# The last token block's gate in pieces of 384 and 128 columns, its output rows weighted early and stored from two queues

## The chip, the cores and the metric

The kernel runs on one core of a Trainium2 chip. The metric is device time in microseconds (us) of one execution. The profiled execution is one further run, recorded by the hardware profiler; its trace is what the rows below come from.

## The reference

One layer of a streaming encoder on 512 tokens with 1024 channels, in float32: a normalised input projection, two attention branches merged by gates, an MLP, then a gated per-layer embedding and a final norm. Only the end of it matters here:

```
ple_gate = sigmoid(rms_norm(h, g_ple) @ w_ple_gate)      # 512x1024 @ 1024x1024
h   = h + ple_gate * (p @ w_ple_proj)
out = rms_norm(h, g_final)                               # h * rsqrt(mean(h*h) + eps) * g_final
```

The output, 512 x 1024 float32, is 2 MB.

## The kernel before

The 512 tokens are four blocks of 128 (`NT` = 4; `LT` = 3 is the last one), one token to a partition. A float32 product is made of three matmuls in a 4-byte format that TensorE takes at full rate: each operand is split into a high and a low part, and `mm3` (lines 74 to 76) adds high x high, high x low and low x high in PSUM.

The gate product of a block is made for 512 columns at a time: 8 slices of the contraction x 3 matmuls = 24 matmuls of 512 columns, each with its own 128x128 weight load (the tokens are the stationary operand). First all four blocks' columns 0 to 511, then columns 512 to 1023 of blocks 0, 1 and 2 (`psgt` in the profile). The last block's columns 512 to 1023 are made in two pieces of 256 (`gate_piece`, `psgl` in the profile), each of 24 matmuls.

What follows a piece (`merge`, `merge_ssq`):

- ScalarE (ACT): sigmoid of the PSUM piece, scaled by the row factor of the earlier norm (line 1398).
- VectorE (DVE): times the projected embedding `pp` (line 1399), then added into `h_sb` (line 1400).
- ACT: square of the new `h_sb` with the row sum into one column of `acc4[tb]` (line 1404, an ACTIVATE and a short read of the accumulator).

`finish(tb)` ends a block: GpSimd (POOL) makes the factor `rs` = (sum + eps)^-0.5 in two small operations (`rms_rstd`, lines 359 and 362), DVE multiplies `h_sb`, `rs` and the broadcast weights `gb4` in one instruction for each half row (line 1423), and SyncE (SP) stores each half, 256 KB (line 1425). The last block has its own end: its first 512 columns are multiplied by `gb4` early (line 1442); when `rs` is there (lines 1452 and 1454), DVE scales those 512 columns (line 1456), then multiplies columns 512 to 767 by both (line 1458); ACT scales columns 768 to 1023 (line 1461) and DVE multiplies these by `gb4` (line 1462). SP stores the two halves (lines 1457 and 1463).

Here the order of instructions on PE, POOL, ACT and DVE is that of the program text (`manual_schedule`). In that text `finish(LT - 1)`, the end of block 2, stands between the first and the second piece of the last block. Line 1488 is the program's closing part, where the engines wait for the last stores and for each other.

Of the kernel before, what the change touches and what calls it, by code (L numbers as in the profile page):

```python
# [8 lines left out]
F32 = mybir.dt.float32  # L9
F32R = mybir.dt.float32r  # L10
AF = mybir.ActivationFunctionType
ALU = mybir.AluOpType
PSUM = bass.MemoryType.PSUM

P = 128
S = 512
# [34 lines left out]
def layer_kernel(ctx: ExitStack, tc: tile.TileContext, x, p, g_mix, w_in, b_forget, swa_sinks,  # L51
                 w_br_swa, w_br_fox, w_mix_out, g_mlp, w_ff1, w_ff2, g_ple, w_ple_gate,
                 w_ple_proj, g_final, out):
    nc = tc.nc
# [3 lines left out]
    out = out[0]  # L58
# [820 lines left out]
    def mm_tile(name, tg=None):  # L879
        if tg is None:  # L880
            n_mm[0] += 1
            tg = ("mm", "sc", "sc", "mm", "sc")[n_mm[0] % 5]
        return psA.tile([P, S], F32, tag=tg, bufs=2 if tg == "mm" else 3, name=name)
# [344 lines left out]
    u3 = {}  # L1228
# [162 lines left out]
    gb4 = hp.tile([P, D], F32, tag="gb", bufs=1, name="g_final_bc")  # L1391
    bcast_row(gb4, g_final)

    def merge(tb, ps, c0, n):

        sl = slice(c0, c0 + n)
        sg = wk3.tile([P, S], F32, tag="tmp", bufs=7, name=f"sgp_{tb}_{c0}")
        nc.scalar.activation(sg[:, 0:n], ps, AF.Sigmoid, scale=rs3[:, tb:tb + 1])  # L1398
        nc.vector.tensor_tensor(sg[:, 0:n], sg[:, 0:n], pp[tb][:, sl], ALU.mult)  # L1399
        nc.vector.tensor_tensor(h_sb[:, tb, sl], h_sb[:, tb, sl], sg[:, 0:n], ALU.add)  # L1400
        return sg
# [2 lines left out]
        nc.scalar.activation(sg[:, 0:n], h_sb[:, tb, c0:c0 + n], AF.Square, scale=1.0 / 32,  # L1404
                             accum_out=acc4[tb][:, col:col + 1])

    def gate_piece(tb, q):

        ts_ = slice(tb * P, (tb + 1) * P)
        ps = mm_tile(f"psgl_{q}")  # L1410
        for k in range(KT):
            wh, wl = unit(("pg", 1, k // 2))
            sl = slice(q * 256, q * 256 + 256)
            mm3(ps[:, 0:256], u3["h"][:, k, ts_], u3["l"][:, k, ts_], wh[:, k % 2, sl],
                wl[:, k % 2, sl], k == 0, k == KT - 1)
        return ps[:, 0:256]

    def finish(tb):
        o = wk3.tile([P, D], F32, tag="xn", bufs=2, name=f"o_{tb}")
# [14 lines left out]
    with tc.manual_schedule(engines={ET.Activation, ET.DVE}):  # L1434
        for tb in range(LT):
            ps = row_group("psgt", "pg", u3_t, 1, tb)
            if tb > 0:
                finish(tb - 1)
            sg = merge(tb, ps, 512, 512)
            merge_ssq(tb, sg, 512, 512, 1)  # L1440
        o = wk3.tile([P, D], F32, tag="xn", bufs=2, name=f"o_{LT}")
        nc.vector.tensor_tensor(o[:, 0:512], h_sb[:, LT, 0:512], gb4[:, 0:512], ALU.mult)
        ps0, ps1 = gate_piece(LT, 0), gate_piece(LT, 1)
        sg = merge(LT, ps0, 512, 256)
        merge_ssq(LT, sg, 512, 256, 1)
        finish(LT - 1)
        acc = acc4[LT]
        nc.vector.tensor_tensor(acc[:, 0:1], acc[:, 0:1], acc[:, 1:2], ALU.add)
        sg = merge(LT, ps1, 768, 256)
        merge_ssq(LT, sg, 768, 256, 2)  # L1450
        ms = sm.tile([P, 1], F32, tag="ms", name="n4_l_ms")
        nc.gpsimd.tensor_scalar(ms, acc[:, 0:1], acc[:, 2:3], EPS, ALU.add, ALU.add)
        rs = sm.tile([P, 1], F32, tag="rs", name="n4_l_rs")
        nc.gpsimd.tensor_tensor(rs, ms, mhalf, ALU.pow)
        rows_ = slice(LT * P, (LT + 1) * P)
        nc.vector.tensor_scalar(o[:, 0:512], o[:, 0:512], rs, None, ALU.mult)
        nc.sync.dma_start(out[rows_, 0:512], o[:, 0:512])
        nc.vector.scalar_tensor_tensor(o[:, 512:768], h_sb[:, LT, 512:768], rs, gb4[:, 512:768],
                                       ALU.mult, ALU.mult)
        hg = sg[:, 256:512]  # L1460
        nc.scalar.activation(hg, h_sb[:, LT, 768:1024], AF.Copy, scale=rs)
        nc.vector.tensor_tensor(o[:, 768:1024], hg, gb4[:, 768:1024], ALU.mult)
        nc.sync.dma_start(out[rows_, 512:1024], o[:, 512:1024])


# [27 lines left out]
```

## Time and profile before

| | us |
|---|---|
| median of 3 runs (lowest, highest) | 721.35 (721.29, 721.50) |
| profiled execution | 721.84 |
| its span, first to last instruction | 720.1 |
| PE busy in the span | 705.6 (98%) |
| DVE, ACT, POOL busy | 531.5, 449.4, 87.6 |

1.74 us of the profiled execution lie outside its span. A line of a timeline gives the start in the span, the duration, the engine, the line of the kernel, the operation, and output <- inputs. "SPq" and "ACTq" are the instruction queues of SyncE and ScalarE, from which stores are issued. A busy PE is not PE at its peak, since the ends of matmuls are modelled.

### The profile page before, as it was taken

The numbers are of one execution on the slowest core, as the hardware profiler recorded it, in microseconds if no ns is written. First come the engines' busy times: TensorE is split into PE (matmuls) and PEld (weight loads), VectorE is DVE, ScalarE is ACT, GpSimd is POOL, SyncE is SP. The second block draws the span as 40 slices with busy tenths as digits, with TensorE's granted clock in tenths as the row PEclk, the third lists the DMA queues.
The fourth block names the chain that finished last, engine by engine and source line by source line (L and its number), as shares of the span: only waits on it lengthen the run. The fifth ranks groups of instructions, "written<-read, shape, count | busy, mean of one in ns | idle before, by whom it ended". The sixth has DMA issues, their size and how long they took to land.

```text
span 720.1 us, 11455 instructions
## 1 busy us (share of the span) xinstructions
PE 705.6 (98%) x4229; PEld 626.6 (87%) x4229; DVE 531.5 (74%) x900; ACT 449.4 (62%) x836; POOL 87.6 (12%) x127
## 2 busy tenths in 40 slices
PE   7999999999999999999999999999999999999995
PEld 6988888888888998888899789988999889988884
DVE  5567888877696556545879985899679966997564
ACT  5547888779863553344777646874578546866452
POOL 1011211100001200002410102010300020010101
PEclk9999999999999999999999999999999999999998
DMA  9256456670364894450995598739994689079002
GB/s 290 65 155 159 109 136 154 150 197 1 118 206 116 152 339 162 160 173 11 252 220 202 105 285 168 235 87 254 190 259 113 157 234 227 31 147 349 1 30 87
DMA packets 74055, 116.72 MB, mean 162 GB/s; under 512 B 6664, under 2 KB 44048, under 8 KB 74000
## 3 DMA queue, kind: packets, MB, share of 16 engines
q1 hardware_dynamic: 65792, 86.38, 37.9%
q0 software_dynamic: 8064, 29.36, 22.2%
q8 instruction: 33, 0.54, 0.3%
q10 hardware_dynamic: 144, 0.26, 0.1%
q14 instruction: 22, 0.18, 0.1%
HBM read 72.93 MB, written 4.19 MB: 107 GB/s over the span
## 4 chain that ended last, share of the span: by engine, by line
PE 85%; DVE 9%; ACT 2%; issue 2%; DMA 1%; POOL 0%; POOLq 0%; DVEq 0%; ACTq 0%
PE pf L74 5%; PE pf L76 5%; PE pf L75 5%; PE s_6x L1309 3%; PE s_4x L1309 3%; PE s_0x L1309 3%; PE s_2x L1309 3%; PE h_sc L752 2%; PE h_pv L822 2%; PE h_tr L810 2%; PE psy L75 2%; PE psy L76 2%; PE psy L74 2%; PE psm L76 2%; PE psm L75 2%; PE psm L74 2%
## 5 line engine op out<-in xcount | busy, mean ns | idle before, releaser
L298 POOL DMA_DIRECT2D wq<-wq x26 | 23.6, 942 | 174.9 <-DVE u154l L325 25.9
L770 ACT ACTIVATE s<-s,h_nm 128x128 f32<-128x128 f32 (+1 forms) x64 | 32.6, 512 | 5.9 <-DVE h_nm L763 5.1
L359 POOL TENSOR_SCALAR n_ms<-acc 128x1 f32<-128x1 f32 x15 | 6.3, 419 | 164.8 <-ACT junk L1075 100.4
L71 DVE TENSOR_TENSOR h_ptl<-h_tr,h_pth 128x512 fp32r<-128x512 f32 (+2 forms) x40 | 22.9, 604 | 3.9 <-ACT h_pth L70 3.6
L467 PE MATMUL va<-wv_h,u 128*128 128x320 f32 x64 | 20.1, 319 | 0.8 <-ACT u L70 0.7
L70 ACT CAST h_pth<-h_tr 128x512 fp32r<-128x512 f32 (+2 forms) x40 | 19.4, 523 | 1.8 <-PE h_tr L810 1.4
L70 ACT CAST u<-n_tr 128x512 fp32r<-128x512 f32 x22 | 12.2, 586 | 13.1 <-PE n_tr L1123 5.9
L810 PE MATMUL h_tr<-ident,s 128*128 128x128 f32 x136 | 19.6, 277 | 0.2
L467 PE MATMUL vb<-wv_h,u 128*128 128x328 f32 x64 | 19.6, 313 | 0.0
L298 POOL DMA_DIRECT2D wgw<-wgw x8 | 7.1, 970 | 101.9 <-DVE u25l L325 77.7
L71 DVE TENSOR_TENSOR u<-n_tr,u 128x512 fp32r<-128x512 f32 x22 | 14.6, 685 | 6.5 <-ACT u L70 6.5
L1075 ACT ACTIVATE junk<-h_sb 128x512 f32<-128x512 f32 x16 | 10.1, 630 | 12.3 <-DVE h_sb L1065 9.8
L822 PE MATMUL h_pv<-h_pth,v 128*128 128x256 f32 (+1 forms) x64 | 17.3, 291 | 0.0
L822 PE MATMUL h_pv<-h_ptl,v 128*128 128x256 f32 (+1 forms) x64 | 16.9, 305 | 0.3 <-DVE h_ptl L71 0.3
L810 PEld LDWEIGHTS h_tr<-ident,s 128*128 128x128 f32 x136 | 15.0, 141 | 2.0 <-ACT s L790 0.5
L1399 DVE TENSOR_TENSOR sgp<-sgp,pp 128x512 f32<-128x512 f32 (+1 forms) x9 | 5.7, 633 | 14.6 <-ACT sgp L1398 14.6
L1065 DVE TENSOR_TENSOR h_sb<-psm,h_sb 128x512 f32<-128x512 f32 x8 | 5.5, 689 | 14.3 <-PE psm L76 14.3
L790 ACT ACTIVATE s<-s,h_rec 128x128 f32<-128x128 f32 (+2 forms) x32 | 14.2, 482 | 2.3 <-DVE h_rec L784 2.3
L832 DVE TENSOR_TENSOR h_ao<-h_pv,h_ao 64x512 f32<-64x512 f32 x16 | 10.9, 681 | 6.1 <-ACT h_ao L831 5.8
L758 DVE CUSTOM_DVE_ANT_0 s<-h_sc,causal 128x128 f32<-128x128 f32 (+3 forms) x32 | 13.8, 482 | 0.3 <-PE h_sc L752 0.3
L784 DVE RECIPROCAL h_rec<-h_den 128x4 f32<-128x4 f32 x16 | 3.0, 185 | 14.5 <-ACT s L770 14.3
L822 PEld LDWEIGHTS h_pv<-h_ptl,v 128*128 128x128 f32 x64 | 12.1, 188 | 1.7 <-DVE h_ptl L71 0.8
(1607 smaller groups left out, 2773.8 us busy)
## 6 DMA issues: line engine op xcount, KB each, us to landing
wq<-in_w_ff_dram SPq DMA_DIRECT2D x45, 512.0 KB, 5.7
wq<-wq POOLq DMA_DIRECT2D x26, 512.0 KB, 5.1
wq_c<-in_w_ff_dram SPq DMA_DIRECT2D x9, 512.0 KB, 5.8
wg<-in_w_in_dram SPq DMA_DIRECT2D x4, 1024.0 KB, 5.4
wgw<-in_w_in_dram SPq DMA_DIRECT2D x8, 512.0 KB, 5.2
wgw<-wgw POOLq DMA_DIRECT2D x8, 512.0 KB, 5.8
wmix<-in_w_mix_out_dram SPq DMA_DIRECT2D x4, 1024.0 KB, 4.9
wpg<-in_w_ple_gate_dram SPq DMA_DIRECT2D x4, 1024.0 KB, 8.6
```

What stands on the lines that cost most here:

```text
L70: nc.scalar.copy(hi, src)
L71: nc.vector.tensor_tensor(lo, src, hi.bitcast(F32), ALU.subtract)
L74: nc.tensor.matmul(ps, lh, rh, start=start, stop=False)
L75: nc.tensor.matmul(ps, lh, rl, start=False, stop=False)
L76: nc.tensor.matmul(ps, ll, rh, start=False, stop=stop)
L298: nc.gpsimd.dma_start(q, other, accum_op=ALU.add)
L467: nc.tensor.matmul(ps, u[:, kk_, ts_], w[:, kk_, c0:c1], start=kk_ == 0 and n == 0, stop=kk_ == KT - 1 and n == 2)
L752: nc.tensor.matmul(ps[:, off:off + n], qs[i][z][:, qb * P:(qb + 1) * P], kk[i][z][:, k0:k0 + n], start=z == 0, stop=z == 1)
L770: nc.scalar.activation(sl, sl, AF.Exp, bias=nm[:, qb:qb + 1], accum_out=den[:, qb:qb + 1])
L810: nc.tensor.transpose(tr[:, n, :], c["s"][:, o, :], ident)
L822: nc.tensor.matmul(pv[:, q0:q0 + nq, :], V2[kb][:, c["v"], :], t[:, o:o + nq, :], start=n == 0, stop=n == 2 * NT - 1, skip_group_check=True)
L1309: nc.tensor.matmul(ps, o[:, j, ts_], w[:, j, :], start=tg != "" and j == 0 and n == 0, stop=j == 1 and n == 2, skip_group_check=True)
```

## The change

The last block's second half of the gate is cut at column 384 instead of 256. `gate`, the sigmoid, is taken out of `merge`, so that the second piece's sigmoid stands ahead of the first piece's square on ACT. Columns 512 to 1023 of the last block's rows are multiplied by `gb4` on DVE piece by piece, before the row factor is known. `finish(LT - 1)` stands behind all of this. When the factor is there, ACT scales columns 0 to 511 and stores them from its own queue, and DVE scales columns 512 to 1023, which SP stores.

```diff
-    def merge(tb, ps, c0, n):
-
-        sl = slice(c0, c0 + n)
+    def gate(tb, ps, c0, n):
         sg = wk3.tile([P, S], F32, tag="tmp", bufs=7, name=f"sgp_{tb}_{c0}")
         nc.scalar.activation(sg[:, 0:n], ps, AF.Sigmoid, scale=rs3[:, tb:tb + 1])
+        return sg
+
+    def merge(tb, ps, c0, n, sg=None):
+
+        sl = slice(c0, c0 + n)
+        if sg is None:
+            sg = gate(tb, ps, c0, n)
...
-    def gate_piece(tb, q):
+    def gate_piece(tb, c0, c1):
...
-        ps = mm_tile(f"psgl_{q}")
+        ps = mm_tile(f"psgl_{c0}")[:, 0:c1 - c0]
...
-        ps0, ps1 = gate_piece(LT, 0), gate_piece(LT, 1)
-        sg = merge(LT, ps0, 512, 256)
-        merge_ssq(LT, sg, 512, 256, 1)
-        finish(LT - 1)
+        C = 384
+        ps0, ps1 = gate_piece(LT, 0, C), gate_piece(LT, C, 512)
+        sg = merge(LT, ps0, 512, C)
+        sg1 = gate(LT, ps1, 512 + C, 512 - C)
+        merge_ssq(LT, sg, 512, C, 1)
+        nc.vector.tensor_tensor(o[:, 512:512 + C], h_sb[:, LT, 512:512 + C], gb4[:, 512:512 + C],
+                                ALU.mult)
+        merge(LT, ps1, 512 + C, 512 - C, sg1)
         acc = acc4[LT]
         nc.vector.tensor_tensor(acc[:, 0:1], acc[:, 0:1], acc[:, 1:2], ALU.add)
-        sg = merge(LT, ps1, 768, 256)
-        merge_ssq(LT, sg, 768, 256, 2)
+        merge_ssq(LT, sg1, 512 + C, 512 - C, 2)
+        nc.vector.tensor_tensor(o[:, 512 + C:], h_sb[:, LT, 512 + C:], gb4[:, 512 + C:], ALU.mult)
+        finish(LT - 1)
...
-        nc.vector.tensor_scalar(o[:, 0:512], o[:, 0:512], rs, None, ALU.mult)
-        nc.sync.dma_start(out[rows_, 0:512], o[:, 0:512])
-        nc.vector.scalar_tensor_tensor(o[:, 512:768], h_sb[:, LT, 512:768], rs, gb4[:, 512:768],
-                                       ALU.mult, ALU.mult)
-        hg = sg[:, 256:512]
-        nc.scalar.activation(hg, h_sb[:, LT, 768:1024], AF.Copy, scale=rs)
-        nc.vector.tensor_tensor(o[:, 768:1024], hg, gb4[:, 768:1024], ALU.mult)
+        nc.scalar.activation(o[:, 0:512], o[:, 0:512], AF.Copy, scale=rs)
+        nc.scalar.dma_start(out[rows_, 0:512], o[:, 0:512])
+        nc.vector.tensor_scalar(o[:, 512:1024], o[:, 512:1024], rs, None, ALU.mult)
         nc.sync.dma_start(out[rows_, 512:1024], o[:, 512:1024])
```

## Rows read from the trace of the kernel before

**Rows 1.** The page, its fourth part: the chain of work that ended last, shares of the span by engine.

```profile
PE 85%; DVE 9%; ACT 2%; issue 2%; DMA 1%; POOL 0%; POOLq 0%; DVEq 0%; ACTq 0%
```

**Rows 2.** The chain that ended last, from 705 us to the end, in order of time: start, duration, engine, output and line. Between the first two rows here lie the other matmuls of the two pieces.

```profile
705.85 0.11 PE psgl L74
...
711.49 0.13 PE psgl L76
...
711.70 0.48 ACT sgp L1398
...
712.21 0.43 DVE sgp L1399
...
712.66 0.43 DVE h_sb L1400
...
713.12 0.52 ACT sgp L1404 x2
...
713.73 0.30 POOL n_l_ms L1452
...
714.07 0.61 POOLq L1488
```

**Rows 3.** The timeline from 707.2 us to the end, all engines; "x2" are two instructions in one row, and its time runs from the first's start to the second's end.

```profile
710.13 1.41 DVE L1423 SCALAR_TENSOR_TENSOR o<-h_sb,n_rs,g_final_bc 128x512 f32<-128x512 f32 x2
...
710.91 0.99 SPq L1425 DMA_DIRECT2D out_dram<-o  x2
...
711.46 0.15 DVE L1448 TENSOR_TENSOR acc<-acc 128x1 f32<-128x1 f32 x1
...
714.71 0.51 ACT L1461 ACTIVATE sgp<-h_sb,n_l_rs 128x256 f32<-128x256 f32 x1 [1.08 <-POOL n_l_rs L1454]
714.71 0.48 DVE L1456 TENSOR_SCALAR o<-o,n_l_rs 128x512 f32<-128x512 f32 x1 [1.62 <-POOL n_l_rs L1454]
715.11 0.48 DVE L1458 SCALAR_TENSOR_TENSOR o<-h_sb,n_l_rs,g_final_bc 128x256 f32<-128x256 f32 x1
715.22 0.33 SPq L1457 DMA_DIRECT2D out_dram<-o  x1
715.51 0.42 DVE L1462 TENSOR_TENSOR o<-sgp,g_final_bc 128x256 f32<-128x256 f32 x1
715.95 0.33 SPq L1463 DMA_DIRECT2D out_dram<-o  x1
```

**Rows 4.** The timeline of an attention head from 195 us, PE and its weight loads (PEld): matmuls of the same 4-byte format, with a new 128x128 weight load each, of 384, 256 and 128 columns, and the first of 512 columns behind them.

```profile
195.40 0.34 PE L822 MATMUL h_pv<-h_pth,v 128*128 128x384 f32 x1
...
195.58 0.34 PE L822 MATMUL h_pv<-h_ptl,v 128*128 128x384 f32 x1
...
195.75 0.28 PE L822 MATMUL h_pv<-h_pth,v 128*128 128x256 f32 x1
...
195.99 0.23 PE L822 MATMUL h_pv<-h_pth,v 128*128 128x128 f32 x1
195.99 0.19 PEld L822 LDWEIGHTS h_pv<-h_ptl,v 128*128 128x128 f32 x1
196.05 0.27 PE L822 MATMUL h_pv<-h_ptl,v 128*128 128x128 f32 x1
196.10 0.19 PEld L74 LDWEIGHTS pf<-u,u18h 128*128 128x128 f32 x1
196.16 0.44 PE L74 MATMUL pf<-u,u18h 128*128 128x512 f32 x1
```

**Rows 5.** The instructions on the sigmoid's tile, 690 us to the end: count, duration in ns (min/median/max), first and last start, and the shapes among them.

```profile
L1399 DVE TENSOR_TENSOR sgp<-sgp,pp x6: 424/691/693, 690.8 to 712.2; 128x512 f32<-128x512 f32 x4, 128x256 f32<-128x256 f32 x2
...
L1404 ACT ACTIVATE sgp<-h_sb x6: 416/632/634, 692.8 to 713.1; 128x512 f32<-128x512 f32 x4, 128x256 f32<-128x256 f32 x2
L1404 ACT ACTIVATION_READ_ACCUMULATOR sgp<-h_sb x6: 185/186/187, 693.3 to 713.4; 128x1 f32 x6
L1398 ACT ACTIVATE sgp<-psgt,rs x4: 670/691/693, 689.9 to 705.9; 128x512 f32<-128x512 f32 x4
L1398 ACT ACTIVATE sgp<-psgl,rs x2: 474/474/475, 708.8 to 711.7; 128x256 f32<-128x256 f32 x2
```

**Rows 6.** Stretches of 0.25 and 1 us around the last four stores: the stretch, its length, busy time of each engine (instructions), then the granted TensorE clock, the mean busy share of the 16 DMA engines and what they moved in GB/s.

```profile
711.50:711.75 0.25, 0.10 (x1) 0.00 (x0) 0.11 (x2) 0.05 (x1) 0.00 (x0) 1.00 0.06 25
...
712.00:713.00 1.00, 0.00 (x0) 0.00 (x0) 0.76 (x2) 0.17 (x1) 0.00 (x0) 1.00 1.01 377
713.00:713.25 0.25, 0.00 (x0) 0.00 (x0) 0.09 (x1) 0.13 (x1) 0.00 (x0) 1.00 0.52 189
716.00:716.25 0.25, 0.00 (x0) 0.00 (x0) 0.00 (x0) 0.00 (x0) 0.00 (x0) 0.68 0.77 295
716.25:717.25 1.00, 0.00 (x0) 0.00 (x0) 0.00 (x0) 0.00 (x0) 0.00 (x0) 0.50 0.97 361
...
717.50:717.75 0.25, 0.00 (x0) 0.00 (x0) 0.00 (x0) 0.00 (x0) 0.00 (x0) 0.50 0.10 33
```

**Rows 7.** The stores of the output rows from 690 us on, from issue to landing.

```profile
DMA to landing us min/median/max: 2.0/2.0/2.1
```

**Rows 8.** The issues of transfers over the whole kernel, the only one from ACT's queue: output <- input, queue, count, size of each, us from issue to landing.

```profile
x<-in_x_dram ACTq DMA_DIRECT2D x1, 256.0 KB, 3.5
```

More of the change, by code (lines that the diff above doesn't have):

```diff
@@ L1405, in merge_ssq @@
                              accum_out=acc4[tb][:, col:col + 1])
-    def gate_piece(tb, q):
+    def gate_piece(tb, c0, c1):
         ts_ = slice(tb * P, (tb + 1) * P)
-        ps = mm_tile(f"psgl_{q}")
+        ps = mm_tile(f"psgl_{c0}")[:, 0:c1 - c0]
         for k in range(KT):
             wh, wl = unit(("pg", 1, k // 2))
-            sl = slice(q * 256, q * 256 + 256)
-            mm3(ps[:, 0:256], u3["h"][:, k, ts_], u3["l"][:, k, ts_], wh[:, k % 2, sl],
+            sl = slice(c0, c1)
+            mm3(ps, u3["h"][:, k, ts_], u3["l"][:, k, ts_], wh[:, k % 2, sl],
                 wl[:, k % 2, sl], k == 0, k == KT - 1)
-        return ps[:, 0:256]
+        return ps
     def finish(tb):
```

## The prediction

> **What bounds the kernel now.** I read the page first. The chain that ended last is 85% PE and 9% DVE [rows 1], so most of the 720 us is matmul time that the change leaves alone. The question is the end: what lies behind the last matmul, and what the change does to the matmuls just before it. The chain in order of time [rows 2] shows PE running without a gap from the first 256-column matmul of the last block (705.85) to the last (711.49 + 0.13 = 711.62): 48 matmuls, 0.12 us each. Then single instructions take turns: sigmoid 711.70, two DVE steps, square 713.12, two POOL steps to 714.68. The timeline [rows 3] has the rest: DVE and ACT start at 714.71 with the factor; the first store is issued at 715.22, the second at 715.95. A store lands 2.0 us after its issue [rows 7], so the second lands at 717.95; 2.15 us of closing part follow, to 720.1.
>
> The view that decides is the stretches around the stores [rows 6]. From 716.25 to 717.25 the DMA engines are busy 0.97 of the time and move 361 GB/s; the pair of block 2's stores before it, issued at 710.91 and 0.66 later [rows 3], shows 1.01 and 377 GB/s. So a pair of 256 KB stores already fills the engines. Block 2's pair moves from about 711.73 (25 of 377 GB/s in the quarter that ends at 711.75) to 713.12 (189 GB/s in the next quarter): 1.39 us, **0.695 us for a store**, first bytes 0.82 us after the issue. The last pair begins at 716.06, 0.84 after its issue, and its last byte is at 717.52 (33 GB/s in the last quarter).
>
> **The change part by part.** I keep one clock, that of the trace.
>
> *Pieces of 384 and 128 columns.* Before: 48 x 0.12 = 5.77 us. The attention head has the same kind of matmul with its own weight load [rows 4]. 384 columns: starts 195.40, 195.58, 195.75, so 0.175 each, 24 x 0.175 = 4.20 us. 128 columns: the first is followed after 0.06 us (195.99 to 196.05), but the second takes 0.27 instead of 0.23 and the next matmul starts 0.11 behind it (196.16), itself lengthened to 0.44. The weight loads beside them start 0.11 apart (195.99, 196.10). I read that as: the first of the pair found its weights loaded behind a longer matmul, the second had to wait for its own, and a row of 24 such matmuls goes at the pace of the weight loads. Bounds: 24 x 0.06 = 1.44 and 24 x 0.12 = 2.88 (the pace at 256 columns, which bounds it from above); I take 0.11, the row's, 2.64 us. Sum 6.84 instead of 5.77: PE ends at 712.69, **1.07 later**.
>
> The Trainium skill bears on this in "TensorE: Matmul & The Clock Gate". Section "LDWEIGHTS (loading the stationary operand)" gives columns / 1.2 in ns, 107 ns for 128 columns, which is the 0.11 of the rows; section "Back-to-back issue gap" gives about 81 ns for a matmul of 128 columns in a stream of load and matmul pairs. By the first the piece would take 24 x 0.107 = 2.57 us, by the second 24 x 0.081 = 1.94 us.
>
> *The chain behind the piece.* The second piece is half as wide. From 512 and 256 columns [rows 5]: sigmoid 0.691 and 0.474, so 0.366 for 128, 0.11 saved; the DVE steps 0.691 and 0.424, so 0.29, 0.13 saved on each of two; square 0.632 and 0.416, so 0.31, 0.11 saved. Together 0.48. The sigmoid starts 1.07 later, at 712.77; the factor is there at 714.68 + 1.07 - 0.48 = 715.27.
>
> *The new wait.* The second piece's sigmoid now waits for PE until 712.77 on ACT; the first piece's square is queued behind it. The first piece's last addition ends at about 711.9 (705.85 + 4.20, sigmoid from 710.13 for 0.58, two DVE steps of 0.56), so the square loses 1.2 us. It runs 713.14 to 713.76 (0.52 and the accumulator read of 0.19, overlapped by about 0.1). The DVE sum of `acc` waits for it, and behind that the rest of DVE; but DVE's own addition for the second piece ends only at 713.78. Cost: nothing, covered by those DVE steps; without that cover, up to 0.6.
>
> *Early weights.* The product of 384 columns (0.56) lies on DVE between 711.9 and the second sigmoid's end at 713.14: hidden; without the gap it would delay the second piece by 0.56. The product of 128 columns (0.29, of which some 0.08 overlaps the next instruction) stands at 713.95, behind the `acc` sum (0.15), in POOL's time; POOL hides it from the factor, but not from what follows on DVE.
>
> *`finish(LT - 1)` moved.* Its factor has long been there; its two DVE instructions now start at about 714.20 instead of 710.13. By the old rows a pair lasts 1.41, the second 0.66 behind the first, and the first store is issued 0.78 after the start, the second 0.66 later [rows 3]. So block 2's stores are issued at **714.98 and 715.64** on SP, not at 710.91 and 711.57. This is all that moves on SP's queue: the last block's store stands behind both. DVE is taken until about 715.6.
>
> *The last pass.* Before: from 714.71 to the second issue 715.95. After: DVE scales 512 columns (0.48) from 715.52, where the second instruction of `finish` lets it in (0.66 behind that one's start at 714.86), 0.25 later than the factor would allow; SP issues at 716.03. ACT scales 512 columns from 715.30; 256 took 0.51 [rows 3], and 0.22 for 256 more by the sigmoid's step [rows 5], so 0.73; ACT issues at about 716.06. If only the issue mattered, the last store would land at 716.06 + 2.0 = 718.06: 0.11 later than before.
>
> *The DMA engines.* But now four stores, 1 MB, are issued between 714.98 and 716.06. First bytes at 714.98 + 0.83 = 715.81, four times 0.695 makes 2.78, so the last byte moves at 718.59; before, at 717.52. All four are issued early enough to keep the engines full (the last may start at 716.9, while two stores last until 717.2). **Sum: +1.07 us.** The share of 1.0 with one queue leaves no room that a second queue could use. No row has stores from two queues at once. The Trainium skill, "DMA: Bandwidth & Descriptors", section "Issuing engines are not separate DMA queues", says that transfers from several issuers run on the same 16 engines and that a second issuer saves only the time to initiate.
>
> So the profiled execution, 721.84, becomes 722.9. It lies 0.49 above the median of the runs; on the median, 721.35 + 1.07 = **722.4**. 0.2%, about what a measurement of this kernel can tell from no change, is 1.44 us.
>
> **The rivals.**
>
> *A. The 128-column matmuls run faster than 0.11.* At the lower bound, 0.06, PE ends at 711.49. The second sigmoid runs 711.57 to 711.94, then DVE's early product of 384 columns is in the way (until about 712.4); the second addition ends at 712.98 instead of 713.78, and all behind it comes 0.8 earlier: block 2's first store at 714.18, last byte at 717.79, +0.27, 721.6. Speaks for it: the one step of 0.06 in the rows; against it: the lengthened matmul behind it. At the 81 ns that the Trainium skill's "Back-to-back issue gap" gives, the addition ends at 713.08 and the sum is about +0.37, 721.7.
>
> *B. Two queues move more than one.* If the stores didn't hold each other up, only the issue would count: +0.11, 721.5. Against it: shares of 0.97 to 1.01 with one queue. With A as well, the last issue at about 715.26 lands at 717.26, 0.7 earlier, 720.7: the only way to a gain, and still under 0.2%.
>
> *C. The store from ACT's queue lands late.* The kernel's only transfer from that queue, a load at the start, took 3.5 us [rows 8]. A store that takes 3.5 from 716.06 lands at 719.56, 1.61 after the old 717.95: 723.0, slower by over 0.2%. It decides from a landing of 719.39 on, 3.33 us after the issue. For it: the row; against it: that is a load, and SP's stores land in 2.0 [rows 7]; but in my sum, where the four stores share the engines, this one takes about 2.9 already.
>
> **How the numbers follow.** My forecast 0.66: 722.4, with a range of its own from 722.0 to 722.8 (0.1 us for the matmul pace up to 0.12, 0.2 for the stores' rate, the rest the runs' own spread). A 0.13, B 0.06 (both at once 0.02 of these), C 0.15. Faster by over 0.2%: 0.03, left for what none of these names. Slower: C but for its milder half-cases, 0.12, and 0.07 of the forecast's and others' upper tail, together 0.19. Within 0.2%: 0.78. The range reaches down to B and A, 721.5, and up to C, 723.1.
>
> **What would show it.** In the profile after: 24 matmuls of 128 columns start 0.11 apart, PE's last ends at about 712.7; ACT's square of 384 columns starts behind the 128-column sigmoid; block 2's DVE pair begins near 714.2; four stores issued within 1.1 us, DMA share about 1 from 715.8 to 718.6, and the closing part as long as before. A PE end at 711.5 speaks for A, a DMA rate over 390 GB/s for B, a store of ACT's queue that lands last and alone for C. The prediction is wrong if block 2's stores are issued before the last block's second addition, if the closing part grows with a second queue in use, or if the stores of two queues slow each other below 361 GB/s: at 0.79 us each instead of 0.695, the sum passes 0.2%.

## The result and the profile after

The changed kernel takes 723.19 us (median of 9 runs, 722.89 to 724.29) beside 721.83 (median of 9, 721.29 to 723.18) of the kernel before in the same session: ratio 1.0023, 95% interval [1.0014, 1.0032], that is +1.66 us [1.0, 2.3]. The two medians by themselves lie 1.36 us apart, inside the same interval. I had forecast 722.4 and a range up to 723.1, and that no difference of 0.2% would show. Part of the miss is the base: the forecast stands on 721.35, the median of three runs, which are the first three of these nine; the same +1.07 on 721.83 is 722.90. What is left is that the direction of my sum was right and its size was too small. The runs below show that two of its steps were wrong and that a third cost was missing.

The profiled execution after: 723.10 us, span 721.06. Everything that follows is told from the first matmul of the last block's pieces, 705.69 before and 705.45 after: the work ahead of it is the same, and in the kernels below it starts anywhere between 704.69 and 705.97. From there to the end of the span ("the stretch") it is 720.12 - 705.69 = 14.43 us before and 721.06 - 705.45 = **15.61 us** after, +1.18 (the trace holds the span to the nanosecond; the views print it to a tenth). Outside the span lie 723.10 - 721.06 = 2.04 us, before 1.72. So the profiled executions differ by 1.18 - 0.24 (the earlier start) + 0.32 = 1.26.

The timeline of the changed kernel, PE's last matmuls and what follows (start, duration, engine, line, operation, output <- inputs); it answers to [rows 2, 3, 4]:

```profile
709.63 0.22 PE L74 MATMUL psgl<-u169h,u 128*128 128x128 f32 x1
709.70 0.27 PE L75 MATMUL psgl<-u169l,u 128*128 128x128 f32 x1
709.81 0.27 PE L76 MATMUL psgl<-u169h,u 128*128 128x128 f32 x1
...
712.15 0.28 PE L76 MATMUL psgl<-u172h,u 128*128 128x128 f32 x1
...
712.52 0.37 ACT L1396 ACTIVATE sgp<-psgl,rs 128x128 f32<-128x128 f32 x1 [2.05 <-PE psgl L76]
712.79 0.51 ACT L1409 ACTIVATE sgp<-h_sb 128x384 f32<-128x384 f32 x1
713.25 0.29 DVE L1405 TENSOR_TENSOR h_sb<-h_sb,sgp 128x128 f32<-128x128 f32 x1
713.46 0.15 DVE L1457 TENSOR_TENSOR acc<-acc 128x1 f32<-128x1 f32 x1
713.58 0.31 ACT L1409 ACTIVATE sgp<-h_sb 128x128 f32<-128x128 f32 x1 [0.18 <-DVE h_sb L1405]
713.79 1.41 DVE L1428 SCALAR_TENSOR_TENSOR o<-h_sb,n_rs,g_final_bc 128x512 f32<-128x512 f32 x2
714.07 0.62 POOL L1462 TENSOR_SCALAR n_l_ms<-acc 128x1 f32<-128x1 f32 x1 [4.48 <-ACT sgp L1409]
714.56 1.00 SPq L1430 DMA_DIRECT2D out_dram<-o  x2
714.78 0.84 POOL L1464 TENSOR_TENSOR n_l_rs<-n_l_ms,mhalf 128x1 f32<-128x1 f32 x1
715.65 0.72 ACT L1466 ACTIVATE o<-o,n_l_rs 128x512 f32<-128x512 f32 x1 [1.68 <-POOL n_l_rs L1464]
715.65 0.49 DVE L1468 TENSOR_SCALAR o<-o,n_l_rs 128x512 f32<-128x512 f32 x1 [0.45 <-POOL n_l_rs L1464]
716.17 0.33 SPq L1469 DMA_DIRECT2D out_dram<-o  x1
716.40 0.35 ACTq L1467 DMA_DIRECT2D out_dram<-o  x1
```

The matmuls of 128 columns start 0.11 us apart, and PE's part, the sigmoid and the two additions stand where the prediction put them. The row to look at is POOL's: its two operations on one number to a partition took 0.62 and 0.84 us, where the same two operations took 0.30 and 0.56 before:

```profile
713.73 0.30 POOL L1452 TENSOR_SCALAR n_l_ms<-acc 128x1 f32<-128x1 f32 x1 [3.90 <-ACT sgp L1404]
714.11 0.56 POOL L1454 TENSOR_TENSOR n_l_rs<-n_l_ms,mhalf 128x1 f32<-128x1 f32 x1
```

Stretches around the four stores, after (columns as in [rows 6]):

```profile
715.25:715.50 0.25, 0.00 (x0) 0.00 (x0) 0.00 (x0) 0.00 (x0) 0.25 (x1) 0.50 0.43 164
...
716.75:717.00 0.25, 0.00 (x0) 0.00 (x0) 0.00 (x0) 0.00 (x0) 0.00 (x0) 0.50 0.20 66
...
717.25:718.25 1.00, 0.00 (x0) 0.00 (x0) 0.00 (x0) 0.00 (x0) 0.00 (x0) 0.50 1.01 389
718.25:718.50 0.25, 0.00 (x0) 0.00 (x0) 0.00 (x0) 0.00 (x0) 0.00 (x0) 0.50 0.53 197
```

The last byte moves at about 718.4; with the earlier start taken off, the prediction's 718.59 is 718.35. That agreement is chance in part: the first bytes move at about 715.4, some 0.2 us earlier than the sum had them (715.81 less 0.24), since DVE's pair begins at 713.79 and not at 714.20 less 0.24. About as much is lost in the quarter at 66 GB/s, because the factor came late and the last two stores with it. And the last byte was not what the end waited for. That is in the closing line's own rows, which the prediction did not use. DRAIN and EVENT_SEMAPHORE are instructions of that line; the second kind carries the signals between the engines. The closing line of the kernel before, its queues (count, duration in ns min/median/max, first and last start):

```profile
L1488 POOLq EVENT_SEMAPHORE  x4: 17/17/17, 719.4 to 720.0; - x4
L1488 POOLq DRAIN  x3: 40/102/5266, 714.1 to 719.9; - x3
L1488 SPq DRAIN  x3: 7/7/7, 718.5 to 719.6; - x3
```

and of the kernel after:

```profile
L1494 POOLq EVENT_SEMAPHORE  x4: 17/17/17, 720.3 to 721.0; - x4
L1494 POOLq DRAIN  x3: 40/93/5542, 714.7 to 720.8; - x3
L1494 SPq DRAIN  x3: 7/7/7, 719.0 to 720.5; - x3
```

SP waits for its stores and reaches its first DRAIN at 718.5 before and 719.0 after. POOL's first DRAIN begins beside its last operation, lasts 5.27 and 5.54 us, and POOL's first signal comes only at 719.4 and 720.3: 0.9 and 1.3 us after SP was through its stores. In both kernels the end of the span lies 5.44 to 5.45 us behind the end of POOL's last operation (714.67 to 720.12; 715.62 to 721.06).

### The profile page after: what moved, and what is told of

The parts are those of the page before. It is cut to its first block, busy times and chain, and to the rows that moved or that the text cites. A ratio compares the mean times of both kernels' runs of the same rounds, so it can differ in the third digit from the quotient of the medians.

```text
span 721.1 us, 11457 instructions
## 1 busy us (share of the span) xinstructions
PE 706.0 (98%) x4229; PEld 627.0 (87%) x4229; DVE 531.3 (74%) x900; ACT 449.2 (62%) x836; POOL 88.2 (12%) x127
## 4 chain that ended last, share of the span: by engine, by line
PE 88%; DVE 7%; DMA 2%; ACT 1%; issue 1%; POOL 0%; SPq 0%; POOLq 0%; DVEq 0%; ACTq 0%
PE pf L74 5%; PE pf L76 5%; PE pf L75 5%; PE s_6x L1309 3%; PE s_4x L1309 3%; PE s_2x L1309 3%; PE s_0x L1309 3%; PE h_sc L752 2%; PE h_pv L822 2%; PE h_tr L810 2%; PE psm L76 2%; PE psm L75 2%; PE psy L74 2%; PE psy L76 2%; PE psm L74 2%; PE psy L75 2%
## 5 line engine op out<-in xcount | busy, mean ns | idle before, releaser
L1404 DVE TENSOR_TENSOR sgp<-sgp,pp 128x512 f32<-128x512 f32 (+2 forms) x9 | 5.7, 632 | 16.1 <-ACT sgp L1396 16.1
L467 PEld LDWEIGHTS va<-wv_h,u 128*128 128x128 f32 x64 | 12.0, 188 | 2.1 <-ACT u L70 1.4
```

Of the source, the lines that this page charges most:

```text
L467: nc.tensor.matmul(ps, u[:, kk_, ts_], w[:, kk_, c0:c1], start=kk_ == 0 and n == 0, stop=kk_ == KT - 1 and n == 2)
```

## The experiments

In every kernel here the numbers are of the profiled execution, the ratio of the timed runs against runs of the kernel before on the same chip. "Outside" is the time outside the span, the median over the runs of that kernel. The ratio is the one on record; it differs by up to 0.0004 from the quotient of the two medians.

| kernel | stretch | POOL's two last operations | end of POOL's last to end of span | outside | ratio [95%] |
|---|---|---|---|---|---|
| before | 14.43 | 0.30, 0.56 | 5.45 | 1.70 | 1 |
| after | 15.61 | 0.62, 0.84 | 5.44 | 2.07 | 1.0023 [1.0014, 1.0032] |
| s1_sp_queue | 15.62 | 0.62, 0.84 | 5.45 | 1.77 | 1.0022 [1.0013, 1.0031] |
| b1_act_queue | 14.43 | 0.30, 0.56 | 5.44 | 2.06 | 1.0004 [0.9995, 1.0012] |
| f1_finish_early | 15.01 | 0.30, 0.56 | 5.44 | 1.88 | 1.0012 [1.0003, 1.0021] |
| p1_psum_scale | 15.01 | 0.30, 0.56 | 5.44 | 2.07 | 1.0009 [1.0000, 1.0018] |
| d1_pool_later | 15.94 | 0.19 (an added one) | 5.44 | 1.71 | 1.0021 [1.0012, 1.0030] |
| d2_store_later | 14.43 | 0.30, 0.56 | 5.45 | 1.73 | 0.9997 [0.9988, 1.0006] |
| k1_pair_only | 15.61 | 0.62, 0.84 | 5.44 | 2.05 | 1.0019 [1.0010, 1.0028] |
| c1_cut_256 | 15.05 | 0.65, 0.84 | 5.45 | 2.05 | 1.0011 [1.0002, 1.0021] |
| v1_weights_early | 14.42 | 0.30, 0.56 | 5.44 | 1.76 | 1.0000 [0.9991, 1.0009] |
| x1_factor_act | 13.59 | none at the end | - | 1.69 | 0.9990 [0.9981, 0.9999] |
| x2_both | 14.58 | none at the end | - | 1.85 | 1.0001 [0.9992, 1.0010] |
| x3_three_stores | 13.60 | none at the end | - | 1.78 | 0.9993 [0.9984, 1.0002] |

### The queue, the place of block 2's end, POOL's neighbours

Four kernels went first, while I still took the end for that of the stores.

**s1_sp_queue**: the changed kernel with all stores on SP.

```diff
         nc.scalar.activation(o[:, 0:512], o[:, 0:512], AF.Copy, scale=rs)
-        nc.scalar.dma_start(out[rows_, 0:512], o[:, 0:512])
         nc.vector.tensor_scalar(o[:, 512:1024], o[:, 512:1024], rs, None, ALU.mult)
         nc.sync.dma_start(out[rows_, 512:1024], o[:, 512:1024])
+        nc.sync.dma_start(out[rows_, 0:512], o[:, 0:512])
```

> The kernel after with one edit: the last block's columns 0 to 511, still scaled on ACT, are stored from SP behind the other half instead of from ACT's queue. In the kernel after, the stretch from the first matmul of the last block's pieces to the end of the span is 15.7 us (14.4 before), the closing part from the last landing to the end 2.3 (2.15 before), and 2.0 to 2.1 us of an execution lie outside its span (1.74 in the profiled one before). Theory: the second queue in use at the end costs 0.15 us of closing part and 0.3 us outside the span; then this kernel has 2.15 and 1.75, its last store is issued at most 0.1 later, and it is 0.3 to 0.4 us faster than the kernel after, ratio to before about 1.0017. Rival: these two differences are chance from one execution to the next; then the kernel stays within 0.1 us of the kernel after, or gets slower by the later issue.

Measured: stretch 15.62 (after 15.61), 1.77 outside the span instead of 2.07, ratio 1.0022. So half of the theory held: the queue changes nothing inside the span, and the 0.3 us outside come off, but are too small to show in the ratio.

**b1_act_queue**: the kernel before with its last store on ACT's queue.

```diff
-        nc.sync.dma_start(out[rows_, 512:1024], o[:, 512:1024])
+        nc.scalar.dma_start(out[rows_, 512:1024], o[:, 512:1024])
```

> The kernel before with one edit: the last store, columns 512 to 1023 of the last block, is issued from ACT's queue instead of SP's. Nothing is computed in another place or order. Theory of the second queue's cost: the closing part grows from 2.15 to 2.3 us and the time outside the span from 1.74 to about 2.05; 0.4 to 0.5 us slower than before in all, ratio 1.0006. Rival (chance): both as before within 0.05 us, ratio 1.000.

Measured: stretch 14.43, as before to the hundredth; outside the span 2.06 (2.01 to 2.11 in 11 runs) instead of 1.70 (1.66 to 1.77 in 32 of before). So the store from ACT's queue costs 0.36 us, all of it outside the span. In the ratio that is 1.0004, within its uncertainty.

**f1_finish_early**: the changed kernel with `finish(LT - 1)` ahead of the last block's two pieces, so that block 2's multiplications and stores come early.

```diff
         ps0, ps1 = gate_piece(LT, 0, C), gate_piece(LT, C, 512)
+        finish(LT - 1)
         sg = merge(LT, ps0, 512, C)
...
         nc.vector.tensor_tensor(o[:, 512 + C:], h_sb[:, LT, 512 + C:], gb4[:, 512 + C:], ALU.mult)
-        finish(LT - 1)
```

> The kernel after with one edit: the end of block 2 (two DVE multiplications and their two stores) stands ahead of the last block's first piece, where DVE is idle for 2.1 us, instead of behind everything. Theory: in the kernel after, each of POOL's two operations for the last factor waits out one of these DVE multiplications, which read two tensors from SBUF (0.62 and 0.84 us instead of 0.30 and 0.56); here they take 0.30 and 0.56 again, the factor comes 0.60 earlier, only two stores are left at the end, and the last byte moves 0.57 earlier: stretch of 15.1 us, ratio to before about 1.0015. The product for the first piece starts 0.45 later on DVE, which costs nothing. Rival (the late stores alone held the end, POOL's operations were long for another reason, such as the work on ACT beside them): POOL's operations stay at 0.62 and 0.84 and the gain is below 0.1 us.

Measured: stretch 15.01, 0.60 less than after; ratio 1.0012. POOL's two operations are short again, in the timeline of f1:

```profile
714.04 0.30 POOL L1462 TENSOR_SCALAR n_l_ms<-acc 128x1 f32<-128x1 f32 x1 [4.48 <-ACT sgp L1409]
714.43 0.56 POOL L1464 TENSOR_TENSOR n_l_rs<-n_l_ms,mhalf 128x1 f32<-128x1 f32 x1
```

But this moves the two late stores and the two late multiplications together, so it doesn't tell them apart.

**p1_psum_scale**: keeps the two late stores, and a late pair of DVE instructions, but not their two inputs from SBUF, the engines' shared memory. Block 2's rows are multiplied by the weights early, into two tiles in PSUM, the memory that TensorE writes; late, DVE only scales these by the factor.

```diff
+        o2 = wk3.tile([P, D], F32, tag="xn", bufs=2, name=f"o_{LT - 1}")
+        rs2 = rms_rstd(acc4[LT - 1], f"n4_{LT - 1}")
+        hg2 = [psA.tile([P, S], F32, tag="tr", bufs=3, name=f"hg_{i}") for i in range(2)]
+        for i in range(2):
+            nc.vector.tensor_tensor(hg2[i], h_sb[:, LT - 1, i * 512:i * 512 + 512],
+                                    gb4[:, i * 512:i * 512 + 512], ALU.mult)
+
+        def finish_late():
+            for i in range(2):
+                s2 = slice(i * 512, i * 512 + 512)
+                nc.vector.tensor_scalar(o2[:, s2], hg2[i], rs2, None, ALU.mult)
+                nc.sync.dma_start(out[(LT - 1) * P:LT * P, s2], o2[:, s2])
+
...
-        finish(LT - 1)
+        finish_late()
```

> The kernel after, with block 2's rows multiplied by the final weights early on DVE into two PSUM tiles; the late step, at the same place as in the kernel after, is a scaling that reads PSUM (one input, no second tensor from SBUF) and writes the rows, and the stores stay late. Theory (a DVE instruction with two SBUF inputs keeps POOL out): POOL's two operations take 0.30 and 0.56 and the factor comes 0.60 earlier than in the kernel after, although DVE is as busy; the four stores then hold the end: the last byte moves at most 0.3 earlier, since 1 MB at 0.695 us for 256 KB has to pass from block 2's first store on. Stretch 15.4 us. Rivals: any DVE work beside POOL slows it (0.62 and 0.84 stay); or the stores don't hold each other up (then the whole 0.57 is gained, stretch 15.1).

Measured: stretch 15.01, ratio 1.0009. DVE's late pair starts at the same place and lasts as long as in the changed kernel, and POOL beside it is not held up:

```profile
713.33 1.40 DVE L1460 TENSOR_SCALAR o<-hg,n_rs 128x512 f32<-128x512 f32 x2
...
713.62 0.30 POOL L1475 TENSOR_SCALAR n_l_ms<-acc 128x1 f32<-128x1 f32 x1 [3.74 <-ACT sgp L1409]
714.01 0.56 POOL L1477 TENSOR_TENSOR n_l_rs<-n_l_ms,mhalf 128x1 f32<-128x1 f32 x1
714.11 0.99 SPq L1461 DMA_DIRECT2D out_dram<-o  x2
```

The same run has the opposite case, earlier: the two products into PSUM, which do read two SBUF inputs, stand beside POOL's first operation for block 2's factor.

```profile
707.86 1.30 DVE L1454 TENSOR_TENSOR hg<-h_sb,g_final_bc 128x512 f32<-128x512 f32 x2
...
708.20 1.04 POOL L359 TENSOR_SCALAR n_ms<-acc 128x1 f32<-128x1 f32 x1 [4.49 <-ACT sgp L1409]
```

It took 1.04 us instead of 0.30. So what goes with the longer time is DVE's two inputs from SBUF, not a busy DVE and not the place of the result.

The length of the stretch didn't fit my theory. The four stores are all late here, their bytes move without a gap, and the last byte comes some 0.4 us later in the stretch than in f1 (about 12.8 against 12.4 us); by the stores p1 had to be the slower one. Yet both end at 15.01. The rival that named 15.1 was near in the number and not in the reason: the four stores do hold each other up, 1 MB moving from 714.9 to 717.8. What the two have in common is POOL's last operation, and that is how the second theory came up: **the end of the span is POOL's last operation plus 5.44 us, and the stores have time to spare.** The rival to it remained that the last landing sets the end.

### Which of the two sets the end

**d1_pool_later**: the kernel before with one more POOL operation behind its last DVE instruction, an addition on 128x1 whose result nobody uses.

```diff
         nc.vector.tensor_tensor(o[:, 768:1024], hg, gb4[:, 768:1024], ALU.mult)
         nc.sync.dma_start(out[rows_, 512:1024], o[:, 512:1024])
+        late = sm.tile([P, 1], F32, tag="ms", name="late")
+        nc.gpsimd.tensor_tensor(late, o[:, 1023:1024], mhalf, ALU.add)
```

> The kernel before with one small operation more: POOL adds a constant to one column of the last block's finished rows (128x1, result unused), so that POOL's last instruction ends some 1.7 us later than before, at about 10.7 us after the first matmul of the last block's pieces instead of 8.98. Nothing else waits for it. Theory (POOL's closing drain ends 4.67 us after POOL's last instruction and, with 0.78 us behind it, sets the end of the execution; the stores have slack): the stretch grows by the same 1.6 to 1.7 us, from 14.4 to 16.1, ratio about 1.0023. Rival, that of the prediction (the last store's landing sets the end): unchanged, 14.4, ratio 1.000.

Measured: POOL's new operation, and the closing line's DRAIN behind it, in the profile of d1:

```profile
715.43 0.19 POOL L1465 TENSOR_TENSOR late<-o,mhalf 128x1 f32<-128x1 f32 x1 [1.33 <-DVE o L1462]
```

```profile
L1490 POOLq DRAIN  x3: 40/93/4889, 715.4 to 720.8; - x3
```

It ends at 715.62, the span at 721.06: 5.44 again. Stretch 15.94, ratio 1.0021. POOL's last operation ends 1.51 us later in the stretch than before, and the stretch is 1.51 longer. An operation of 0.19 us that nothing waits for costs as much as the whole change.

**d2_store_later**: the kernel before with a DVE multiplication into a scratch tile ahead of the last store's producer, so that the store is issued 0.67 us later.

```diff
         nc.scalar.activation(hg, h_sb[:, LT, 768:1024], AF.Copy, scale=rs)
+        scr = wk3.tile([P, S], F32, tag="tmp", bufs=7, name="scr")
+        nc.vector.scalar_tensor_tensor(scr, h_sb[:, LT, 0:512], rs, gb4[:, 0:512], ALU.mult,
+                                       ALU.mult)
         nc.vector.tensor_tensor(o[:, 768:1024], hg, gb4[:, 768:1024], ALU.mult)
```

> The kernel before with one DVE instruction more ahead of the last one: a multiplication of 512 columns into a scratch tile, 0.66 us, so that the last store is issued 0.66 us later. The factor is there by then, POOL has nothing left to do. Rival, that of the prediction (the last store's landing sets the end): the stretch grows by 0.66, from 14.4 to 15.1, ratio 1.0009. Theory (POOL's drain sets the end): SP is through with its waits 0.8 us before the drain ends, so all 0.66 is slack: 14.4, ratio 1.000.

Measured, the two last stores in the timeline of d2:

```profile
714.22 0.33 SPq L1457 DMA_DIRECT2D out_dram<-o  x1
715.62 0.33 SPq L1466 DMA_DIRECT2D out_dram<-o  x1
```

The last store is issued 1.40 us behind the first instead of 0.73 [rows 3], and the stretch is 14.43, the ratio 0.9997: nothing. With d1 this settles it for the kernel before: 0.67 us on the last store are free, and POOL's last operation moves the end one for one.

### The cut and the pair, each by itself

**k1_pair_only**: f1 with two multiplications into scratch tiles in the place where the changed kernel has block 2's; the stores of block 2 stay early.

```diff
+        for i in range(2):
+            scr = wk3.tile([P, S], F32, tag="tmp", bufs=7, name=f"scr_{i}")
+            nc.vector.scalar_tensor_tensor(scr, h_sb[:, LT - 1, i * 512:i * 512 + 512], mhalf,
+                                           gb4[:, i * 512:i * 512 + 512], ALU.mult, ALU.mult)
```

> The kernel with block 2's end moved early, and two DVE multiplications with the same inputs as there, into scratch tiles, at the late place: DVE reads two tensors from SBUF beside POOL's two operations as in the kernel after, but block 2's stores stay early. Theory: POOL's operations take 0.62 and 0.84 us again instead of 0.30 and 0.56, the factor comes 0.60 later than without the pair, and the end with it: stretch 15.6 as in the kernel after, against 15.0 without the pair; so the pair alone, without the stores, is the loss. Rival (the stores of block 2 at the late place lengthen POOL's operations or the end): 0.30 and 0.56, 15.0.

Measured, the timeline of k1:

```profile
714.07 1.41 DVE L1463 SCALAR_TENSOR_TENSOR scr<-h_sb,mhalf,g_final_bc 128x512 f32<-128x512 f32 x2
...
714.36 0.62 POOL L1466 TENSOR_SCALAR n_l_ms<-acc 128x1 f32<-128x1 f32 x1 [4.49 <-ACT sgp L1409]
715.06 0.84 POOL L1468 TENSOR_TENSOR n_l_rs<-n_l_ms,mhalf 128x1 f32<-128x1 f32 x1
```

Stretch 15.61 against 15.01 of f1: the pair alone, without any late store, costs 0.60 us, and it costs it on POOL (0.62 + 0.84 instead of 0.30 + 0.56, +0.60). The two late stores cost nothing (15.61 with and without them).

**c1_cut_256**: the changed kernel with the cut back at 256.

```diff
-        C = 384
+        C = 256
```

> The changed kernel with its last block cut at 256 and 256 columns as before; the four stores, their two queues and the early weights stay. Theory (the end is GpSimd's last operation plus 5.44 us): the last matmul comes 1.07 us earlier, the chain behind it is 0.48 us longer, and the pair of late multiplications on VectorE still holds GpSimd's two small operations up (0.62 and 0.84 us), so GpSimd's power ends some 0.55 us earlier than in the changed kernel: first late matmul to end of span 15.1 us instead of 15.65, outside the span 2.05 us, ratio to before 1.0014. Rival (the four stores set the end): the two late stores come on the same 0.6 us earlier but the transfers of block 2 are still under way, so the end moves by 0.3 us at most, and the closing stretch between the last landing and the end of the span stays as it is in the changed kernel.

Measured: stretch 15.05, ratio 1.0011, POOL 0.65 and 0.84. The cut costs 15.61 - 15.05 = 0.56.

**v1_weights_early**: the kernel before with only the early weights and the scaling on ACT and DVE; the cut is at 256, `finish(LT - 1)` stands between the two pieces, and SP stores both halves.

> The kernel before with the early weights alone: 256 and 256 columns, block 2's finish between the two pieces and both stores of the last block from SP as before, but the last rows take the weights ahead of the factor, and the two halves are then scaled by the factor on ScalarE and VectorE. Theory: the factor on GpSimd comes at the same place as before, so first late matmul to end of span is 14.4 us and the ratio 1.000, although the last store is issued 0.3 to 0.45 us earlier than before. Rival (the last store sets the end): the stretch falls to 14.0 to 14.1 us, ratio 0.9995.

Measured: stretch 14.42, ratio 1.0000. The last store is issued 9.95 us into the stretch instead of 10.26, and nothing comes of it, as in d2. With the queue (b1, s1) and the late stores (k1) out of the question inside the span, four kernels make a square: neither cut nor pair 14.42 (v1), the cut alone 15.01 (f1, +0.59), the pair alone 15.05 (c1, +0.63), both 15.61 (after, +1.19; the sum of the two is 1.22).

### Versions

**x1_factor_act**: the kernel before with the last block's factor taken from POOL: ACT adds and takes the root, DVE the reciprocal. ACT's table for the root is loaded behind the last sigmoid by an early root of a column that is no longer needed.

```diff
+        nc.vector.tensor_scalar(acc[:, 0:1], acc[:, 0:1], EPS, None, ALU.add)
+        nc.scalar.activation(acc[:, 1:2], acc[:, 1:2], AF.Sqrt)
...
-        nc.gpsimd.tensor_scalar(ms, acc[:, 0:1], acc[:, 2:3], EPS, ALU.add, ALU.add)
+        nc.scalar.activation(ms, acc[:, 2:3], AF.Sqrt, bias=acc[:, 0:1])
...
-        nc.gpsimd.tensor_tensor(rs, ms, mhalf, ALU.pow)
+        nc.vector.reciprocal(rs, ms)
```

> The kernel before with the last factor taken off POOL: DVE adds the eps, ACT takes the square root of the sum (its table is loaded behind the last sigmoid, in ACT's idle time, by an unused square root), DVE the reciprocal. POOL's last instruction is then block 2's factor at 709.8 us. Theory (POOL's drain sets the end before): the factor comes within 0.2 us of where it was (the table load of 1.28 us lasts 0.4 longer than ACT's gap, the square root and reciprocal are 0.5 shorter than POOL's two steps), and the end is now set by the stores: 0.6 to 0.8 us faster than before, stretch 13.7, ratio 0.9990. Rival (the stores set the end before as well): only the shift of the factor is seen, 14.2 to 14.6, ratio 1.000.

Measured: the factor is there 8.96 us into the stretch, where it was before (8.98), and still the stretch is 13.59, 0.84 shorter. The closing line of x1:

```profile
L1490 POOLq EVENT_SEMAPHORE  x4: 17/17/17, 718.4 to 719.1; - x4
L1490 POOLq DRAIN  x3: 40/93/5266, 709.1 to 718.9; - x3
L1490 SPq DRAIN  x3: 7/7/7, 718.4 to 718.7; - x3
```

POOL's DRAIN of 5.27 us now begins at 709.1 and is over long before the end; POOL's first signal comes when SP has its stores, at 718.4. In x1 the stores set the end, and in x2 and x3 below too (POOL's first signal at 719.3 and 718.6, SP's first DRAIN at 719.3 and 718.5). Ratio 0.9990 [0.9981, 0.9999]: the only one of these kernels whose interval lies below 1, and only just.

**x2_both**: x1 with the early weights of v1. In writing it I put the sum into `acc` behind the second piece's addition.

```diff
+        merge(LT, ps1, 512 + C, 512 - C, sg1)
         acc = acc4[LT]
         nc.vector.tensor_tensor(acc[:, 0:1], acc[:, 0:1], acc[:, 1:2], ALU.add)
-        sg = merge(LT, ps1, 768, 256)
```

> The kernel before with the early weights as in v1_weights_early and the last factor on ScalarE as in x1_factor_act. Theory: with GpSimd done early, the stores do set the end, and the early weights now show: the last store is issued 0.1 to 0.4 us earlier than in x1_factor_act, the stretch is 13.2 to 13.5 us instead of 13.61, ratio 0.9986. Rival (weights early are worth nothing at the end at all): 13.6 us and 0.9990, as x1_factor_act.

Measured: stretch 14.58, ratio 1.0001, a miss of both expectations. The timeline of x2 shows why:

```profile
712.81 0.15 DVE L1458 TENSOR_TENSOR acc<-acc 128x1 f32<-128x1 f32 x1
...
713.04 1.28 ACT L1460 ACT_TABLE_LOAD   x1 [1.06 <-DVE acc L1458]
```

The early root waits for that sum, and its table load with it: 1.28 us that lie behind the last sigmoid in x1 now stand on the path, and the scaling starts 1.04 us later than in x1. The stretch is 0.99 longer than x1's.

**x3_three_stores**: x2 with the sum back in its place, and three stores instead of two.

```diff
-        nc.scalar.activation(o[:, 0:512], o[:, 0:512], AF.Copy, scale=rs)
-        nc.vector.tensor_scalar(o[:, 512:1024], o[:, 512:1024], rs, None, ALU.mult)
+        nc.scalar.activation(o[:, 256:512], o[:, 256:512], AF.Copy, scale=rs)
+        nc.vector.tensor_scalar(o[:, 0:256], o[:, 0:256], rs, None, ALU.mult)
+        nc.sync.dma_start(out[rows_, 0:256], o[:, 0:256])
+        nc.vector.tensor_scalar(o[:, 512:1024], o[:, 512:1024], rs, None, ALU.mult)
         nc.sync.dma_start(out[rows_, 512:1024], o[:, 512:1024])
-        nc.sync.dma_start(out[rows_, 0:512], o[:, 0:512])
+        nc.sync.dma_start(out[rows_, 256:512], o[:, 256:512])
```

> The kernel before with the last factor on ScalarE as in x1_factor_act (the addition of the partial sums is back ahead of the second piece's addition, so that ScalarE's table load can start behind the last sigmoid), early weights, and the last rows scaled and stored in three parts: 256 columns from VectorE first, then 512 from VectorE, then 256 from ScalarE, all from SP. Theory: the factor is there at about 9.0 us behind the first late matmul as in x1_factor_act; the first store is issued at 9.35 instead of 9.52, the last byte moves some 0.25 us earlier than there, and since GpSimd is done early the end follows it: stretch 13.3 to 13.45 us instead of 13.61, ratio 0.9987. Rival (what is saved in the stores' issue is lost to a third store, or does not reach the end): 13.6 us or more, 0.9990 or above.

Measured: stretch 13.60, ratio 0.9993 [0.9984, 1.0002]; the rival was right. The first store is issued 9.38 us into the stretch (x1: 9.52), but the engines run half dry behind it. One quarter of x3 (columns as in [rows 6]):

```profile
716.30:716.55 0.25, 0.00 (x0) 0.00 (x0) 0.00 (x0) 0.00 (x0) 0.00 (x0) 0.50 0.69 246
```

and the last byte comes where it came in x1 (6.28 us behind the start of the last matmul, x1 6.29). x1 and x3 can't be told apart by these runs; x1 is the smaller change. What the early weights alone are worth once POOL is off the end stays open: x2 lost it to the table load, and x3 changes the stores as well.

## Why the prediction was wrong, step by step

**Right: the pace of 0.11 us and the PE end.** 24 matmuls of 128 columns, 0.11 apart; the last ends at 712.44, the prediction's 712.69 less the 0.24 of the earlier start is 712.45. Rival A (0.06) is out: only the first step is 0.07, the other 22 are 0.11 in the mean (709.70 to 712.15). Of the two figures of the Trainium skill, "TensorE: Matmul & The Clock Gate", the 107 ns that the section "LDWEIGHTS (loading the stationary operand)" gives agrees with these rows (111 ns in the mean), the 81 ns of "Back-to-back issue gap" doesn't.

**Right: the narrower chain and the new wait.** The second sigmoid starts at 712.52 (712.53 by the prediction), the second addition ends at 713.54 (713.54). ACT's square of 384 columns stood behind that sigmoid, at 712.79, and the `acc` sum started at 713.46, before the second square: the wait was free. c1 measures the cut, PE and chain together, at 0.56, f1 beside v1 at 0.59 (the prediction: 1.07 - 0.48 = 0.59).

**Wrong: "the factor is there at 714.68 + 1.07 - 0.48 = 715.27".** It was there at 715.62, where 715.03 would have been the prediction with the earlier start. I moved block 2's two multiplications into POOL's time and asked only what they do to DVE and to the stores, not what they do to POOL. k1 shows this alone: +0.60 us. The trace of before had the case, if not at this place. DVE and POOL at 667 us, in the kernel before:

```profile
666.65 0.68 DVE L1065 TENSOR_TENSOR h_sb<-s_6x,h_sb 128x512 f32<-128x512 f32 x1
666.92 0.30 POOL L359 TENSOR_SCALAR n_ms<-acc 128x1 f32<-128x1 f32 x1 [4.33 <-ACT junk L1075]
667.25 0.74 DVE L316 SCALAR_TENSOR_TENSOR u167l<-wpg,g_ple_t,u167h 128x512 fp32r<-128x512 f32 x1
667.31 1.10 POOL L362 TENSOR_TENSOR rs<-n_ms,mhalf 128x1 f32<-128x1 f32 x1
667.91 0.68 DVE L71 TENSOR_TENSOR u<-n_tr,u 128x512 fp32r<-128x512 f32 x1
668.50 0.92 POOL L359 TENSOR_SCALAR n_ms<-acc 128x1 f32<-128x1 f32 x1
668.51 0.74 DVE L316 SCALAR_TENSOR_TENSOR u168l<-wpg,g_ple_t,u168h 128x512 fp32r<-128x512 f32 x1
```

The same two POOL operations took 1.10 and 0.92 us there instead of 0.56 and 0.30, beside a DVE instruction of the same kind as block 2's. At 666.92, beside a DVE instruction with one of its two inputs in PSUM (`s_6x`, which PE writes), POOL kept its 0.30. The Trainium skill has a rule for this in "SBUF — State Buffer", section "Who interferes with whom": a DVE instruction with two inputs in SBUF contends with a GpSimd instruction that reads SBUF, and of the port pair that the two engines share it says that "it's an exclusive lock". The runs agree on which instructions contend: beside DVE instructions with two SBUF inputs POOL's pair takes 0.62 and 0.84 us (after, s1, k1), beside ones with a single input, in PSUM, 0.30 and 0.56 (p1). The lengths fit a wait: at 667.31 POOL took 0.54 us more than usual, and DVE's next instruction starts 0.60 behind it. That it is the shared ports that it waits for no run shows by itself, and where the POOL operation came first, as in the last section, DVE was not held up.

**Wrong: "2.15 us of closing part follow" the second landing.** The 2.15 us were a difference between two times, not a wait that any row of the prediction shows. The end doesn't follow the landing, it follows POOL's last operation by 5.44 us (d1, d2), and SP was through its stores 0.9 us before POOL. From this step came the whole view that the four stores decide, and with it the "+1.07 us" for the last byte, 718.59 instead of 717.52. The bytes did end at about that time, and +1.07 lies near the +1.18 of the stretch, but that is luck: the one is not the cause of the other. The stores had time to spare, and k1 without the late stores ends like the changed kernel with them. The chain that [rows 2] comes from does not show this: its last row is DVE's queue in the closing line, at 715.59. The closing line's own rows do, with POOL's DRAIN of 5.27 us.

**Missing: a cost outside the span.** b1 measures 0.36 us for one store from ACT's queue at the end, on no engine's timeline. I had put the 1.7 us outside the span down as a constant. Rival C asked whether that store lands late; it landed 2.4 us after its issue, within what the sum gave it, so C is out as I had put it.

**Rival B**, that two queues move more than one, is out: the engines moved 389 GB/s in the fullest stretch of 1 us after, against 361 and 377 before. s1, with one queue, moved 381 in the same place and has the same stretch, so the second queue brought no rate that matters.

So the sum, by its real terms: the cut +0.56 to +0.59, the pair on POOL +0.60 to +0.63, together +1.18 in the span, and some +0.35 outside, +1.5 us, inside the measured +1.66 [1.0, 2.3]. The early weights, the fewer instructions behind the factor and the second queue could not have helped whatever they saved: they shorten a path that isn't the last one (v1: 0.31 us on the last store, 14.42 instead of 14.43).

## What to carry to other kernels

Before pricing a change at a kernel's end, ask what the end waits for, by the closing line's own rows of every engine; here a chain through the factor to the stores looked like the last one, and POOL's DRAIN was. In these kernels POOL's last small operation had 5.44 us behind it, so an engine whose closing is long should be done early: giving the last factor to another engine shortened the stretch by 0.84 us (ratio 0.9990 [0.9981, 0.9999]) where an earlier last store alone gave nothing. And where an instruction is moved on one engine, look in the trace for what the others' instructions took beside its like.

## What the runs showed that I had not expected

POOL's DRAIN in the closing line ends 4.66 or 4.67 us behind its last operation, whatever that operation is (0.19, 0.56 or 0.84 us long), in x1 to x3 too, where that is long before the end. In all eleven kernels whose last POOL operation stands near the end, 0.78 us more follow to the end of the span: 5.44 or 5.45. What POOL does in the 4.67 us no run shows.

The time outside the span isn't a constant: 1.69 to 1.78 in the kernels with stores from SP alone, 2.05 to 2.07 in those with a store from ACT's queue. Two don't fit: f1, with such a store, has 1.88, and x2, without one, 1.85 (1.65 to 2.04 over its runs). b1 shows that the queue alone can cost it; what the cost is, and why these two lie between, is open.

A POOL operation with a small head start is not held up. In the kernel before, one that had started 0.06 us ahead of a DVE instruction with two SBUF inputs kept its 0.56 us, and DVE's 0.42 was not lengthened either:

```profile
709.27 0.56 POOL L362 TENSOR_TENSOR n_rs<-n_ms,mhalf 128x1 f32<-128x1 f32 x1
709.33 0.42 DVE L1399 TENSOR_TENSOR sgp<-sgp,pp 128x256 f32<-128x256 f32 x1 [0.70 <-ACT sgp L1398]
```

With the two starts 0.01 us apart, at 668.50 in the rows further up, POOL took 0.92 instead of 0.30.
